# Three unread products in the idle rounds of the even mixer's hand-woven stages

## The chip, the cores and the metric

The kernel runs on one core of one Trainium2 chip. The metric is the device time in microseconds; the median of repeated runs counts. The engines are TensorE (PE in the profile; PEld is its weight loads), VectorE (DVE), ScalarE (ACT), GpSimd (POOL) and SyncE (SP, which issues most DMAs).

## What is computed

A two-layer backbone over 256 context and 256 latent tokens of width 1024. Layer 0 (even) mixes with RWKV-7 in two directions beside a pooling mixer; layer 1 (odd) with differential attention beside retention. Behind each stands a mixture of 32 gated experts, two per token. The change lies in the even mixer, whose core is this, per head and direction:

```python
def step(S, inp):
    w_t, k_t, v_t, kk_t, b_t = inp[:5]
    sa = jnp.einsum('bhvk,bhk->bhv', S, -kk_t)
    S = S * w_t[:, :, None, :] + sa[..., None] * b_t[:, :, None, :] + v_t[..., None] * k_t[:, :, None, :]
    return S, jnp.einsum('bhvk,bhk->bhv', S, inp[5])
```

Before it the token rows are projected (h @ w_in), shifted and gated; after it come a norm per head, a bonus term, a gate and the output projection.

## The kernel before

All is float32, and nearly all matmuls are plain float32. The even mixer does not scan token by token. It cuts the 512 tokens into eight chunks of 64 and handles two halves of four heads each, in two directions, so there are four units (half, direction). A unit has three steps. `ev_prep` (products at L690, L697, L703, L743 and L752) builds the decayed matrices of every chunk. `ev_solve` (L802, L825) inverts the triangular blocks with many products of 32 rows, 32 columns and 32 elements. `ev_chain` (L871 to L903) carries the state through the eight chunks, three yields for a chunk.

Beside these run projections of weights (`ev_k`, `ev_r`, `ev_v`, `ev_u`, all at L545) and pieces of the adaLN table (`ev_ada`, L269 to L291), which depend on nothing but weights that a ring buffer streams in.

The order of all this is written out by hand. Each step is a Python generator that emits some instructions and yields. `STAGES` is a table of eight entries: the main generators, the fill generators, a rate `per`, and the PSUM banks for fill and for aside products. `weave` (L109) goes round: each main generator once, then as many steps of fill as the rate has made due. Entries are woven one after the other (L447 to L450). Where the fill of an entry has run out, `next(fill, None)` does nothing and the round holds main work alone. A `per` below 1 gives rounds without fill; the last entry's fill outlasts its main generators.

The yields that matter for a count: an `ev_ada` piece has 3, `ev_k`, `ev_r` and `ev_v` 8 each, `ev_turn` 2, `ev_u` 16. `ev_prep` has 26 yields, so it is in its 27th round when it ends; `ev_chain` has 24, `ev_solve` 25.

The fill's first bank is called f; among the stages' generators only fill writes to it. Every engine takes its instructions in the order in which they were emitted, so what is emitted in one round stands on TensorE ahead of what is emitted in the next. `ident` is a 128x128 identity matrix that is loaded once at the start.

The stages of the odd layer are woven by the same function (L1217 to L1237). The expert layer that follows the even mixer streams its weights from HBM.

Of the kernel before, what the change touches and what calls it, by code (L numbers as in the profile page):

```python
# [10 lines left out]
F32 = mybir.dt.float32  # L11
# [94 lines left out]
    return where, arrays  # L106


def weave(main, fill=(), per=1):  # L109

    fill, end, due, main = chain(*fill), object(), 0, list(main)
    while main:
        main = [g for g in main if next(g, end) is not end]
        due += per
        while due >= 1:
            next(fill, None)
            due -= 1
    for _ in fill:
        pass
# [87 lines left out]
class Kernel:  # L207
# [182 lines left out]
    def even(self, xp, seg):  # L390

        nc, tc, I, c = self.nc, self.tc, self.I, self.c
        with ExitStack() as st:
            self.adaw = mp = st.enter_context(tc.tile_pool(name="even", bufs=1))
            self.xp, self.mp = xp, mp
            unit = ExitStack()
            self.up = unit.enter_context(tc.tile_pool(name="unit", bufs=2, side="right"))

            parts = [self.up.tile([128, 8, *shape], F32R, name=n) for n, *shape in
                     (("AB", 8, 64), ("RK0", 2, 64), ("RK1", 2, 64), ("tok0", 128), ("tok1", 128))]  # L400
            parts = [a.rearrange("p a s i -> p (a s i)" if len(a.shape) == 4 else "p a i -> p (a i)") for a in parts]
            parts = [a[:, n:n + 512] for a in parts for n in range(0, a.shape[1], 512)]
            self.hH, self.hL = parts[:8], parts[8:]
            with ExitStack() as s1:
                tp = s1.enter_context(tc.tile_pool(name="evp", bufs=1))
                self.pp = s1.enter_context(tc.tile_pool(name="evpp", bufs=1, space=PSUM))
                self.bank = self.bank_of("fgh")
                self.condition(mp, tp)
                x = self.inputs(tp, nc.sync)
                first = s1.enter_context(tc.tile_pool(name="first", bufs=5))  # L410
                self.stream.early = first, 9, 5
                self.stream.fill()
                hT = self.x_tiles(xp, [2, 512])
                self.hT = [hT[k // 2][:, k % 2] for k in range(8)]
                mix = self.mix_in(tp, self.pp, 0, x, self.cols[0], 5)
                next(mix)
                pieces = [self.ada(*next(self.todo)) for n in range(4)]
                for n in range(5):
                    if n < 4:
                        next(pieces[n])  # L420
                        next(pieces[n])
                    if n == 0:
                        next(mix)
                    if n == 1:
                        parameters = self.parameters(tp)
                        next(parameters)
                        self.constants(mp, "even", ("heads", "upto0", "mask0", "upto1", "mask1", "eye16", "sub2", "subcol", "headsel", *(f"headrow{t}" for t in range(4))))
                        self.constants(mp, "even", [f"sel{i}" for i in range(16)])
                        self.stream.fill()
                    if n == 3:  # L430
                        lora = self.lora(first)
                        next(lora)
                    if n:
                        next(pieces[n - 1])
                next(mix)
                next(lora)
                next(parameters)
            self.hp = st.enter_context(tc.tile_pool(name="half", bufs=1))
            self.wp = st.enter_context(tc.tile_pool(name="evw", bufs=1))
            self.pp = st.enter_context(tc.tile_pool(name="evps", bufs=1, space=PSUM))  # L440
            self.VU = [self.hp.tile([128, 4, 4, 64], F32, name=f"VU{j}") for j in range(2)]
            self.yT01, yT23 = (mp.tile([128, 2, 512], F32, name=f"yT{b}") for b in range(2))
            self.yT = [a[:, b] for a in (self.yT01, yT23) for b in range(2)]
            self.half, self.unit, self.done, self.seg = {}, {}, set(), seg
            self.splits_ = self.ev_splits()
            self.ahead = list(islice(self.splits_, 2))
            self.free_units = unit.close  # L447
            for main, fill, per, banks, aside in self.STAGES:
                self.bank, self.aside = self.bank_of(banks), self.bank_of(aside)
                weave([getattr(self, "ev_" + n)(*a) for n, *a in main], [getattr(self, "ev_" + n)(*a) for n, *a in fill], per)  # L450
        return self.x

    def bank_of(self, names):
# [219 lines left out]
    def ev_prep(self, half, d):  # L673
# [12 lines left out]
        for q in range(2):  # L686
            b = 2 * half + q
            ps = bank([128, 4, 128])
            for t in range(4):
                nc.tensor.matmul(ps[:, t], self.wdT[:, 128 * t:128 * t + 128], self.wup[:, d, 128 * b:128 * b + 128],  # L690
                                 start=t == 0, stop=t == 3, skip_group_check=True)
# [4 lines left out]
            ps = bank([128, 512])  # L696
# [4 lines left out]
            ps = bank([128, 512])  # L701
            for t in range(4):
                nc.tensor.matmul(ps[:, 128 * t:128 * t + 128], lw[:, t], c[f"upto{d}"], start=t == 0, stop=t == 3,  # L703
                                 skip_group_check=True)
# [35 lines left out]
            for n in range(2):  # L740
                ps = bank([128, 4, 128])
# [4 lines left out]
            for n in range(2):  # L746
                for h in range(2):
                    H = slice(64 * h, 64 * h + 64)
                    ps = bank([128, 4, 128])
                    for i in range(4):  # L750
                        ch = 4 * n + i ^ q
                        nc.tensor.matmul(ps[:, i], KB[H, 128 * ch:128 * ch + 128], u["RK"][q][H, ch].rearrange("p s i -> p (s i)"),  # L752
                                         start=i == 0, stop=i == 3, skip_group_check=True)
# [2 lines left out]
                    yield  # L756
        for h in range(2):
            nc.vector.tensor_scalar(u["PH"][:, :, :, h], u["Pe"], c["heads"][:, 64 * h:64 * h + 1], None, op0=ALU.mult)

    def ev_solve(self, half, d):  # L760

# [420 lines left out]
    def odd(self, x, seg):  # L1182

        nc, tc, I = self.nc, self.tc, self.I
        with ExitStack() as st:
# [28 lines left out]
            for g in (self.od_turned("k0", self.kT[0:2], 0), self.od_turned("q0", self.qT[0:2], 256), self.od_tokens("v0", self.V[0])):  # L1214
                for _ in g:
                    pass
            weave([*(self.od_attend(n, 0) for n in range(2)), self.router_weights(self.bank_of(("b6",)))],  # L1217
                  [self.od_turned("k1", self.kT[2:4], 0), self.od_turned("q1", self.qT[2:4], 256), self.od_tokens("v1", self.V[1])], 2)
            self.flush()
            weave([*(self.od_attend(n, 1) for n in range(2)), self.od_heads(0, self.Yr[0], self.ss[0], 1e-5)],  # L1220
                  [self.od_turned("dk", self.dkT, 0), self.od_turned("dq", self.dqT, 256), self.od_tokens("dv0", self.DV[0])], 2)
            self.flush()
# [1377 lines left out]
```

## Time and profile before

| | us |
|---|---|
| median of three runs | 1868.96 |
| lowest, highest | 1865.75, 1869.52 |
| profiled execution, its own time | 1874.16 |
| span from its first to its last instruction | 1872.4 |
| TensorE busy | 1637.9 (87% of the span) |
| VectorE busy | 817.3 (44%) |
| ScalarE busy | 447.0 (24%) |
| mean granted TensorE clock | 0.925 |

The span is what all positions in the profile are counted in, in microseconds from the first instruction. [...] A matmul's time in the profile is from its start until its result is out, and matmuls overlap, so a busy TensorE may still have room; the distance from one group's start to the next one's tells how long it holds the engine. The even mixer goes from about 50 to about 575 us.

### The profile page before, as it was taken

Reading aid. Unit: us, or ns where it says so; the run is one execution under the profiler, and the core shown is the slowest. Engines: PE = TensorE matmul, PEld = TensorE weight load, DVE = VectorE, ACT = ScalarE, POOL = GpSimd, SP = SyncE. Lnnn points to the kernel's source line nnn. Section 1 sums busy time; section 2 is a strip of 40 time slices with the busy share of each in tenths; the row PEclk is TensorE's granted clock in tenths of the full one; section 3 lists DMA queues with packets and bytes.
Section 4 is the critical chain, followed back from the end, with each engine's and each line's share of the span. In section 5 each row is a group of like instructions: output and inputs, shape, how many; then the busy total and the mean of one; then the engine's idle time right before and its main releaser. Section 6 shows DMA issues by size and latency. Waiting matters only on the chain. (4 is left out here: it accounts for less than half of the span.)

```text
span 1872.4 us, 31604 instructions
## 1 busy us (share of the span) xinstructions
PE 1637.9 (87%) x12958; PEld 933.3 (50%) x12958; DVE 817.3 (44%) x1622; ACT 447.0 (24%) x945; POOL 139.5 (7%) x170
## 2 busy tenths in 40 slices
PE   5988999989998999999999997999987787776667
PEld 2755556454776444444444433888754333332222
DVE  2564434544358245555555456665562212221113
ACT  3442222421213211111111112544421111111001
POOL 1021000103115000000000003200010000000001
PEclk8998987879898999999999997999988899898888
DMA  9275300652243879999999990622699998999996
GB/s 319 82 239 191 113 24 23 216 172 92 85 146 141 350 283 386 399 385 390 390 401 379 399 386 12 198 68 85 259 369 413 415 415 318 414 414 414 366 400 253
DMA packets 127284, 505.76 MB, mean 270 GB/s; under 512 B 11317, under 2 KB 38945, under 8 KB 85986
## 3 DMA queue, kind: packets, MB, share of 16 engines
q1 hardware_dynamic: 120946, 493.96, 68.1%
q0 software_dynamic: 3488, 8.26, 1.4%
q8 instruction: 143, 2.34, 0.5%
q10 hardware_dynamic: 2640, 0.65, 0.2%
q14 instruction: 67, 0.55, 0.1%
HBM read 501.73 MB, written 1.10 MB: 269 GB/s over the span
## 5 line engine op out<-in xcount | busy, mean ns | idle before, releaser
L1979 PE MATMUL b<-w,ht 128*64 128x512 f32 x512 | 118.8, 604 | 8.6 <-PEq L2197 8.2
L2004 DVE TENSOR_TENSOR tmp<-b,g 128x512 f32<-128x512 f32 x128 | 87.6, 686 | 70.1 <-PE b L2002 69.2
L1958 PE MATMUL b<-w,xh 128*64 128x512 f32 x512 | 116.9, 599 | 0.0
L1958 PE MATMUL b<-w,xg 128*64 128x512 f32 x512 | 116.9, 599 | 0.0
L2287 PE MATMUL b<-w,x 128*32 128x256 f32 x1024 | 77.8, 430 | 31.7 <-DMA w<-moe_w_up 14.9
L2006 DVE TENSOR_TENSOR x<-x,tmp 128x512 f32<-128x512 f32 x124 | 90.1, 726 | 4.3
L2287 PE MATMUL b<-w,xg 128*32 128x256 f32 x1024 | 74.0, 420 | 19.1 <-DMA w<-moe_w_up 14.4
L1987 DVE TENSOR_TENSOR yl<-b,yh 64x512 fp32r<-64x512 f32 x62 | 42.7, 688 | 101.4 <-ACT yh L1986 101.4
L2304 PE MATMUL b<-w,ht 128*32 128x256 f32 x1024 | 71.2, 415 | 16.6 <-ACT ht L2299 12.4
L2292 DVE SCALAR_TENSOR_TENSOR low<-b,gs,low 64x256 f32<-64x256 f32 x32 | 15.7, 490 | 157.6 <-ACT low L2291 157.6
L1979 PEld LDWEIGHTS b<-w,ht 128*64 128x64 f32 x512 | 41.6, 138 | 84.0 <-issue 72.5
L1962 ACT ACTIVATE low<-b 64x512 f32<-64x512 f32 x33 | 19.4, 588 | 253.9 <-PEq L2197 221.0
L2453 DVE COPY y<-b 32x256 f32<-32x256 f32 x62 | 25.9, 418 | 119.6 <-PE b L2304 106.3
L2287 PEld LDWEIGHTS b<-w,x 128*32 128x32 f32 x1024 | 37.1, 122 | 69.5 <-DMA w<-moe_w_up 20.6
L1986 ACT CAST yh<-b 64x512 fp32r<-64x512 f32 x62 | 36.0, 581 | 127.8 <-PE b L1979 104.6
L1963 DVE SCALAR_TENSOR_TENSOR low<-b,gs,low 64x512 f32<-64x512 f32 x32 | 36.1, 1127 | 67.2 <-ACT low L1962 67.2
L1958 PEld LDWEIGHTS b<-w,xh 128*64 128x64 f32 x512 | 33.9, 136 | 62.6 <-issue 62.0
L1958 PEld LDWEIGHTS b<-w,xg 128*64 128x64 f32 x512 | 33.9, 136 | 62.3 <-issue 61.3
L2291 ACT ACTIVATE low<-b 64x256 f32<-64x256 f32 (+1 forms) x36 | 14.4, 399 | 209.9 <-PEq L2501 130.4
L2287 PEld LDWEIGHTS b<-w,xg 128*32 128x32 f32 x1024 | 36.0, 120 | 53.3 <-DMA w<-moe_w_up 19.5
L2002 PE MATMUL b<-yh,oht 128*128 128x512 f32 (+1 forms) x128 | 58.3, 456 | 3.2 <-DVE tmp L2004 3.2
L1374 PE MATMUL b<-w,hH 128*128 128x256 f32 x320 | 59.4, 286 | 0.0
(868 smaller groups left out, 3115.5 us busy)
## 6 DMA issues: line engine op xcount, KB each, us to landing
w<-moe_w_gate SPq DMA_DIRECT2D x128, 1024.0 KB
w<-moe_w_up SPq DMA_DIRECT2D x128, 1024.0 KB
w<-moe_w_down SPq DMA_DIRECT2D x128, 1024.0 KB
w<-ada_w SPq DMA_DIRECT2D x48, 1024.0 KB
w<-od_w_in SPq DMA_DIRECT2D x12, 1024.0 KB
w<-ev_w_in SPq DMA_DIRECT2D x8, 1024.0 KB
w<-ev_w_out SPq DMA_DIRECT2D x5, 1024.0 KB
w<-od_w_out SPq DMA_DIRECT2D x4, 1024.0 KB
```

What stands on the lines that cost most here:

```text
L1374: nc.tensor.matmul(ps[:, t], l[:, k, T], r[:, k], start=t == 0 and k == 0 and i == 0, stop=k == 7 and i == 2, skip_group_check=True)
L1958: nc.tensor.matmul(ps[64 * j:64 * j + 64], xe(k), w[j][:, k % 4], start=k == 0, stop=k == 7)
L1963: nc.vector.scalar_tensor_tensor(hs[64:128].rearrange("s k q -> s q k"), ps[64:128].rearrange("s (q k) -> s q k", k=4), gs, sg[64:128].rea ...
L1979: nc.tensor.matmul(ps[64 * j:64 * j + 64], ht[:, k], w[:, k % 2, 512 * j:512 * j + 512], start=k == 0, stop=k == 3)
L1986: nc.scalar.copy(out=yh[:, j], in_=pj)
L1987: nc.vector.tensor_tensor(yl[:, j], pj, yh[:, j].bitcast(F32), op=ALU.subtract)
L2002: nc.tensor.matmul(ps, ohT[0:n, t], y[0:n, j], start=i == 0, stop=i == len(parts) - 1)
L2004: nc.vector.tensor_tensor(tmp, ps, g2[seg[t]][:, 512 * j:512 * j + 512], op=ALU.mult)
L2006: (nc.gpsimd if j in aside else nc.vector).tensor_tensor(xs, xs, tmp, op=ALU.add)
L2287: nc.tensor.matmul(ps[groups[j]], xe(k), w[j // 2][:, k % 4, 256 * (j % 2):256 * (j % 2) + 256], start=k == 0, stop=k == 7, skip_group_che ...
L2304: nc.tensor.matmul(ps[groups[j]], ht[:, k % 2, S * (k // 2):S * (k // 2) + S], w[:, k % 2, 256 * j:256 * j + 256], start=k == 0, stop=k == ...
L2453: (nc.scalar.copy if j % 2 else nc.vector.tensor_copy)(out=out, in_=ps[groups[j]])
```

## The change

`weave` gets a function `idle`. It is called where a step of fill is due, the fill has run out, and a main generator is left. For the even mixer's entries it is `ev_idle`, which takes bank f and issues three products of the identity with itself, 128 columns each, into it; nothing reads them. For the entry that has `end` among its main generators, and for the odd layer's stages, it does nothing.

```diff
-def weave(main, fill=(), per=1):
+def weave(main, fill=(), per=1, idle=lambda: None):
...
         while due >= 1:
-            next(fill, None)
+            if next(fill, end) is end and main:
+                idle()
             due -= 1
...
-                weave([getattr(self, "ev_" + n)(*a) for n, *a in main], [getattr(self, "ev_" + n)(*a) for n, *a in fill], per)
+                weave([getattr(self, "ev_" + n)(*a) for n, *a in main], [getattr(self, "ev_" + n)(*a) for n, *a in fill], per,
+                      self.ev_idle if ("end",) not in main else lambda: None)
...
+    def ev_idle(self):
+
+
+        ps = self.pp.tile([128, 512], F32, name="f")
+        for i in range(3):
+            self.nc.tensor.matmul(ps[:, 128 * i:128 * i + 128], self.c["ident"], self.c["ident"], start=i == 0, stop=i == 2, skip_group_check=True)
```

## Rows read from the trace of the kernel before

**Rows 1.** The page's second part: granted clock and DMA share, 40 slices

```profile
PEclk8998987879898999999999997999988899898888
DMA  9275300652243879999999990622699998999996
```

**Rows 2.** Busy time, granted clock, DMA share and GB/s by stretch

```profile
core 0: us, PE busy (x) PEld busy (x) DVE busy (x) ACT busy (x) POOL busy (x), PEclk, DMA share, GB/s
165.00:171.80 6.80, 4.07 (x97) 2.60 (x101) 5.07 (x11) 1.09 (x2) 0.00 (x0) 0.50 0.38 144
178.60:192.20 13.60, 13.60 (x183) 9.24 (x184) 7.03 (x14) 4.96 (x10) 0.36 (x2) 0.50 0.11 27
257.20:270.70 13.50, 12.19 (x139) 7.49 (x133) 2.10 (x4) 5.48 (x9) 0.00 (x0) 0.50 0.06 21
308.40:339.00 30.60, 29.84 (x145) 19.46 (x145) 11.78 (x25) 8.45 (x18) 1.21 (x3) 0.50 0.18 61
383.50:403.80 20.30, 19.03 (x305) 13.92 (x305) 7.50 (x14) 6.64 (x13) 0.57 (x2) 0.50 0.24 81
468.80:485.70 16.90, 15.68 (x217) 11.20 (x211) 3.69 (x8) 7.12 (x14) 4.46 (x7) 0.50 0.51 154
485.90:574.50 88.60, 87.28 (x611) 64.70 (x610) 48.74 (x91) 16.21 (x37) 18.57 (x17) 1.00 0.29 101
575.00:1120.00 545.00, 528.82 (x2624) 250.37 (x2625) 270.55 (x449) 101.40 (x188) 16.42 (x12) 0.98 0.91 364
```

**Rows 3.** Timeline of TensorE: start, length, line, shapes; products and transposes of 128 columns

```profile
118.45 0.66 PE L743 MATMUL p<-const_ident,KB 128*128 128x128 f32 x4 [0.46 <-DVE KB L726]
118.94 0.60 PE L743 MATMUL P<-const_ident,KB 128*128 128x128 f32 x4
...
157.33 1.16 PE L703 MATMUL P<-const_heads,lw 128*128 128x128 f32 x8
158.42 0.99 PE L802 MATMUL s<-A,const_sel 32*32 32x224 f32 x16
...
336.97 1.92 PE L703 MATMUL p<-const_heads,lw 128*128 128x128 f32 x8
338.68 1.14 PE L280 MATMUL c<-const_ident,part 128*128 128x2 f32 x8
```

**Rows 4.** The same timeline, 167 to 183 us; in brackets idle time before, and releaser

```profile
167.73 2.07 PE L920 MATMUL C<-sq,const_heads 128*128 128x512 f32 x2 [3.71 <-DVE sq L916]
...
177.98 0.37 PE L752 MATMUL p<-RK,KB 64*128 64x128 f32 x1 [1.63 <-issue]
...
181.28 2.07 PE L752 MATMUL p<-RK,KB 64*128 64x128 f32 x8
```

**Rows 5.** The same timeline, 254 to 271 us

```profile
254.44 0.33 PE L903 MATMUL y<-AB,VU 128*64 128x64 f32 x2 [0.69 <-ACT VU L884]
...
259.41 1.92 PE L825 MATMUL s<-TT,A 32*32 32x32 f32 x64 [1.31 <-ACT A L845]
...
266.50 3.78 PE L545 MATMUL f<-x,w 128*128 128x512 f32 x4
```

**Rows 6.** The same timeline, 293 to 309 us

```profile
293.70 1.16 PE L752 MATMUL p<-RK,KB 64*128 64x128 f32 x8
294.79 0.46 PE L890 MATMUL C<-VU,tok 128*64 128x64 f32 x8
...
305.96 0.65 PE L890 MATMUL C<-VU,tok 128*64 128x64 f32 x6 [1.09 <-ACT VU L884]
...
308.53 0.70 PE L874 MATMUL c<-ZB,RK 128*64 128x128 f32 x4 [1.18 <-DVE ZB L897]
```

**Rows 7.** The same timeline, breaks and waits around 384 and 468 us

```profile
384.77 1.49 PE L825 MATMUL s<-TT,A 32*32 32x32 f32 x93 [4.23 <-issue]
...
468.11 0.50 PE L825 MATMUL s<-TT,A 32*32 32x32 f32 x35 [3.24 <-issue]
...
477.57 1.92 PE L825 MATMUL s<-TT,A 32*32 32x32 f32 x64 [0.69 <-ACT A L845]
...
480.64 1.05 PE L883 MATMUL C<-R,AB 64*64 64x64 f32 x8 [0.53 <-ACT R L876]
```

## The prediction

> **What bounds the kernel now.** I read the page's slices first. In the first eleven the granted TensorE clock dips again and again while the DMA engines are mostly idle; later the DMA engines are 0.9 busy and more [rows 1]. The even mixer is the first part, so there TensorE and its clock set the pace, and the expert layer behind it, 0.91 busy with DMA, can only start when the mixer has ended [rows 2]. I therefore count a microsecond won or lost in the mixer as one at the end.
>
> Second, the table by stretch, cut where the clock changes [rows 2]. [...]
>
> Third, TensorE's timeline ahead of each fall. The first has a 3.71 us wait for VectorE in front of it, the second a 1.63 us break in which TensorE waited for nothing that the profile shows [rows 4]. The third has waits of 0.69 and 1.31 us around it [rows 5], the fourth waits of 1.09 and 1.18 us [rows 6], the fifth and sixth breaks of 4.23 and 3.24 us [rows 7]. So a fall follows a short hole, and the slow stretch then outlasts the hole by far.
>
> **Where the products go.** I counted the yields. A triple is issued in each round in which the fill has run out and a main generator is left. Entry 2 of STAGES has 27 rounds at 0.8 and 19 fill steps: 1 triple. Entry 3: 27 rounds, 18 steps: 8. Entry 4: 26 and 22: 3. Entry 5: 27 rounds at 0.9 and 8 steps: 15. Entry 6: 27 and 23: 3. Entry 7: 26 and 22: 3. Entries 1 and 8: none. That is 33 triples, 99 products. Nothing is removed or moved, no DMA is added, and bank f was read out a round or more before the first triple of each entry, so no new wait arises. TensorE's queue is in order, though: all that is queued behind a triple is late by its length unless it would have waited anyway.
>
> **The price of one triple.** Four products of this shape appear as eight records and hold TensorE from 157.33 to 158.42, 1.09 us at the full clock; four one-record transposes of 128 columns are followed 0.49 us later by the next four without a gap [rows 3]. Six records cost 0.73 us by the transposes; the group with its closing gap gives 0.82 us for six, and 1.09 us is an upper end. A triple waits for nothing, so it should join the work around it without that gap. I take 0.70, just under the nearest row, with 0.65 and 1.09 as ends. At the half clock the four products take 1.71 us [rows 3], so a triple 1.3 to 1.5; I take 1.4.
>
> **What a held clock is worth.** The same group of eight records lasts 2.07 us at half clock and 1.16 us at full [rows 4, 6]. Work that keeps TensorE busy at half clock thus gives back 0.91 of 2.07, some 0.42 to 0.44 of its time; I use 0.42.
>
> **Entry 2**, one triple near 124 us at full clock. Whether TensorE is late there I did not follow up; +0.3, between 0 and 0.7.
>
> **Entry 3**, eight triples between 164 and 187 us. The first lies in the 3.71 us wait: free. That hole is still some 3 us long, so I let the first fall stand, and the second triple costs 1.4. Six follow at full clock, 4.2, of which I hide 1.5 in the break of 1.63 us [rows 4]. Cost 4.1. Since they stand on both sides of the break, I expect the fall at 178.6 not to come: 0.42 of 13.6 busy us is 5.7 [rows 2]. Net -1.6.
>
> **Entry 4**, three triples between 253 and 261 us. Two lie in the waits of 0.69 (nearly all of it) and 1.31 us [rows 5]; the third costs 0.7. The fall at 257 should not come, since the holes that led to it are filled: 0.42 of 12.19 is 5.1. The large group in it, 3.78 us long [rows 5], can shrink fully, as it waits for nothing. Net -4.4.
>
> **Entry 5**, fifteen triples between 294 and 326 us, is the balance on which the sum hangs. Up to 305 the groups stand back to back: eight records of the preparation from 293.70, the chain's next piece at 294.79, 1.09 us later [rows 6]. Six triples there delay everything. Two lie in the waits of 1.09 and 1.18 us. Seven more follow among back-to-back work. Thirteen paid at 0.70 are 9.1. Against it, the fall at 308 should not come: 0.42 of 29.84 is 12.5. If it stayed away without cover from ScalarE and VectorE, up to 1.5 of this would turn into waits for them, and they would be late next. Net -3.4.
>
> **Entry 6**, three triples behind 392 us. The 4.23 us break comes in a round that still has fill, so nothing is put there and the fall at 383.5 stands; the triples run at half clock, 4.2, and may bring the clock back a little earlier. I take 1.0 for that, between 0 and 0.42 of 10 us. Net +3.2. **Entry 7**: the 3.24 us break is ahead of its triples too. They cost 4.2, of which 1.2 goes into waits of 0.69 and 0.53 us [rows 7]; an earlier rise gives 1.6. Net +1.4.
>
> Sum: 0.3 - 1.6 - 4.4 - 3.4 + 3.2 + 1.4 = -4.5 us. The profiled execution took 1874.16 us for a span of 1872.4, 5.2 us above the median of 1868.96; it would become 1869.7, and the median 1864.5.
>
> [...] The breaks come in front of small products with many instructions each, and a triple adds instructions ahead of them, so a break may move to a better or worse place; from the rows, each is worth between nothing and 4.23 us [rows 7]. The sum leaves them where they are. [...]
>
> **Rivals.**
> *Slower: the clock falls at 178.6 all the same.* Then seven triples of entry 3 are paid at 1.4, 9.8 less 1.5, and nothing comes back: -1.6 becomes +8.3, the sum +5.4, 1874.4 us. For it: a 1.63 us break alone, between busy groups, was enough before, and 32x32 products fill much of that time. Against: a triple stands on each side. It decides from the point at which the clock there is below about 0.75. If the third fall stays too, -4.4 becomes about +2.1 and the time 1881.
> *No change: the triples fit worse.* At 1.09 each, some twenty paid at full clock add 7.8: +3.3, 1872.3; at about 0.9 they add 4 and leave -0.5, 1868.5. For it: every group in the rows has its gap behind it. Against: the transposes have none.
> *A larger gain: a break moves.* Without the fifth fall entry 6 goes from +3.2 to 2.1 less 8.0, -5.9, and the sum to -13.6: 1855.4 us. It hangs on a place that nothing in the change aims at.
> *The change does nothing to the clock* because products nobody reads are dropped, or never issued: 1869. The program writes them to a bank like any other; I give it next to nothing.
>
> **How the numbers follow.** Some 0.2%, 3.7 us, is what a measurement here tells from no change. The forecast, between -9 and 0, has 0.50: 0.34 of it below -3.7, 0.16 within. A worse fit 0.13, all within. A larger gain 0.10. The slower rival 0.27. That makes faster 0.44, same 0.29, slower 0.27. Both signs hold much of the chance; the forecast's own range is 1860 to 1869. The range for all reaches down to the moved break, 1855, and up between the two prices of the slower rival, 1878.
>
> **What would show it.** Right: 1.00 in the stretches that began at 178.6, 257.2 and 308.4; 0.50 again behind the breaks of entries 6 and 7; triples of 0.65 to 0.9 us at full clock; the work from 294 to 305 us longer by some 4 us. Wrong: a triple above 1 us; 0.50 in the fourth stretch, which alone turns -3.4 into a loss of more than 9; or full clock in entry 6.

## The result and the profile after

The changed kernel takes 1884.20 us, the median of six runs (1881.64 to 1890.17); the kernel before, run beside it, 1868.28. The ratio is 1.0086 (95% interval 1.0068 to 1.0103): **slower by 15.9 us**. I had forecast 1864.5 and a range up to 1878.

The page of the changed kernel, its profiled execution (1890.17 us, the slowest of the six):

```profile
span 1888.4 us, 32004 instructions
PE 1652.5 (88%) x13156; PEld 950.7 (50%) x13156; DVE 818.1 (43%) x1622; ACT 446.6 (24%) x945; POOL 140.2 (7%) x170
PEclk8999989979897999999999998999989999887878
q8 instruction: 144, 2.36, 0.5%
```

TensorE has 198 matmuls and 198 weight loads more than before (12958 of each). So the 99 products are 396 instructions: two matmuls and two loads each. In all the page counts 400 more than the 31604 of before; the other four are waits of TensorE on semaphores, in the mixer. The slices of the mixer show more nines than in [rows 1]: the clock is held better (0.931 against 0.925 over the whole kernel), and the kernel is slower all the same. The last slices (eights and nines down to 7878) are no better than before, though the change adds nothing there.

The stretches at 0.50 of the mixer, but for two of 3.4 us at 64.0 and 122.1, by stretch (PE busy, PEld, DVE, ACT, POOL, then granted clock as a share of the full one, DMA share, GB/s):

```profile
173.30:180.10 6.80, 6.01 (x141) 4.59 (x141) 3.59 (x7) 0.58 (x1) 0.00 (x0) 0.50 0.10 37
200.60:204.00 3.40, 3.40 (x38) 1.36 (x41) 0.38 (x2) 0.10 (x1) 0.00 (x0) 0.50 0.80 271
265.40:279.00 13.60, 13.23 (x113) 8.17 (x112) 2.10 (x4) 4.95 (x9) 0.00 (x0) 0.50 0.01 1
350.70:354.10 3.40, 3.40 (x16) 1.66 (x16) 3.29 (x8) 0.27 (x1) 0.57 (x1) 0.51 0.84 317
388.30:415.50 27.20, 24.05 (x350) 18.71 (x350) 7.87 (x14) 7.01 (x14) 0.87 (x2) 0.50 0.22 74
480.50:490.70 10.20, 8.24 (x94) 5.76 (x86) 1.70 (x3) 2.72 (x6) 4.47 (x7) 0.50 0.78 236
```

Against [rows 2]: the 30.6 us of the fifth entry are gone (3.4 left, later), the 13.6 us at 178.6 have become 3.4, the 13.5 us at 257 have stayed, the sixth entry's stretch has grown from 20.3 to 27.2, and the seventh's has shrunk from 16.9 to 10.2.

A triple, and TensorE's breaks, by its timeline (matmuls of `ev_idle` stand on L768, `ev_prep`'s on L746 and L755, the solver's small products on L835):

```profile
130.57 0.94 PE L768 MATMUL f<-const_ident 128*128 128x128 f32 x6
131.43 1.16 PE L755 MATMUL P<-RK,KB 64*128 64x128 f32 x8
...
175.95 1.49 PE L768 MATMUL f<-const_ident 128*128 128x128 f32 x6
177.23 1.06 PE L746 MATMUL p<-const_ident,KB 128*128 128x128 f32 x4
...
303.06 0.94 PE L768 MATMUL f<-const_ident 128*128 128x128 f32 x6
303.92 0.46 PE L900 MATMUL C<-VU,tok 128*64 128x64 f32 x8
...
389.65 1.93 PE L835 MATMUL s<-TT,A 32*32 32x32 f32 x128 [3.40 <-issue]
393.38 1.11 PE L746 MATMUL P<-const_ident,KB 128*128 128x128 f32 x4 [1.80 <-issue]
...
408.60 1.65 PE L768 MATMUL f<-const_ident 128*128 128x128 f32 x6
410.18 2.07 PE L755 MATMUL P<-RK,KB 64*128 64x128 f32 x8
...
479.63 0.96 PE L835 MATMUL s<-TT,A 32*32 32x32 f32 x88 [3.87 <-issue]
```

From the start of a triple to the start of what follows are 0.86 us at the full clock (twice above; the median of all 33) and 1.28 to 1.58 at half (both ends above; 1.58 four times). The breaks, in which TensorE waits for nothing that the profile shows, are not where they were in [rows 4, 7]: sizes and places have moved.

**Where the breaks stand.** I counted every record of TensorE from the start of the trace, those included that the busy columns leave out, up to each break of 0.7 us or more between 100 and 500 us. In the kernel before they come after 2241, 2497, 6849 and 8897 records; in the changed one after 7105, 7361, 9153 and 9409. The remainder modulo 256 is 193 in all of these, and in every one of 71 more such breaks in the eighteen kernels of the experiments. So breaks of this size come there only at every 256th record. I call these places **cuts**, and the 256 records between two of them a block; an inserted instruction moves all later cuts in the program. The 400 added move those behind the mixer by 400 - 256 = 144 places.

In the page's queue "q8 instruction" are 144 packets, 2.36 MB in all and 16.4 KB each. That TensorE waits for them at the cuts I infer from their times. In the kernel before, packets of the queue land at 172.80, 176.66, 383.46 and 466.71 us, and the four breaks end at 174.25, 177.98, 384.77 and 468.11. From the second break to the third, 4352 records, 17 packets land, one for every 256. All 79 breaks end 1.14 to 1.59 us behind a landing, though there are only some 35 landings in the 400 us. No two packets start less than 3.3 us apart there in any trace, while the 256 records ahead of the four breaks were used up in 2.36, 1.83, 2.70 and 2.68 us. In all traces 65 of the 79 breaks follow a block used up in less than 3.3 us, and only 35 of the 633 cuts without such a break do. So a cut shows as a break mostly where a block falls into dense small products that are through in less than the 3.3 us between two packets.

**The end of the kernel** shows the loss where nothing was added. The latest and longest of TensorE's waits for "issue" or its own sequencer (PEq) in the last 70 us; first the kernel before, then the changed one:

```profile
1842.48 0.41 PE L2311 MATMUL b<-const_ident,oh 128*128 128x128 f32 x2 [0.30 <-PEq L2501]
1850.49 3.67 PE L2518 MATMUL b<-y,oht 96*128 96x512 f32 x8 [0.31 <-PEq L2501]
```

```profile
1821.35 3.04 PE L2329 MATMUL b<-y,oht 128*128 128x512 f32 x6 [1.18 <-issue]
1857.30 0.41 PE L2321 MATMUL b<-const_ident,oh 128*128 128x128 f32 x2 [0.30 <-PEq L2511]
1862.46 3.21 PE L2297 MATMUL b<-w,x 128*32 128x256 f32 x51 [0.79 <-issue]
1866.49 3.67 PE L2528 MATMUL b<-y,oht 96*128 96x512 f32 x8 [0.81 <-PEq L2511]
```

The 19 waits of this kind of 0.7 us or more after 1790 us, in all traces, end 1.28 to 1.86 us behind the landing of an instruction packet.

From one and the same VectorE instruction (a `low` addition, L2292 before and L2302 after, at 1738.50 and 1751.22 us) to the end are 133.9 us before and 137.2 after. I call this the **end segment** below.

### The profile page after: what moved, and what is told of

It reads as the page before. It is cut to its first block, busy times and chain, and to the rows that moved or that the text cites. A ratio compares the mean times of both kernels' runs of the same rounds, so it can differ in the third digit from the quotient of the medians.

```text
span 1888.4 us, 32004 instructions
## 1 busy us (share of the span) xinstructions
PE 1652.5 (88%) x13156; PEld 950.7 (50%) x13156; DVE 818.1 (43%) x1622; ACT 446.6 (24%) x945; POOL 140.2 (7%) x170
## 3 DMA queue, kind: packets, MB, share of 16 engines
q8 instruction: 144, 2.36, 0.5%
## 5 line engine op out<-in xcount | busy, mean ns | idle before, releaser
L2297 PE MATMUL b<-w,x 128*32 128x256 f32 x1024 | 76.9, 419 | 29.2 <-DMA w<-moe_w_up 13.5
L2314 PE MATMUL b<-w,ht 128*32 128x256 f32 x1024 | 75.0, 430 | 17.3 <-ACT ht L2309 12.5
L2302 DVE SCALAR_TENSOR_TENSOR low<-b,gs,low 64x256 f32<-64x256 f32 x32 | 15.7, 491 | 147.4 <-ACT low L2301 147.4
```

The costliest lines, as they stand in the source:

```text
L2297: nc.tensor.matmul(ps[groups[j]], xe(k), w[j // 2][:, k % 4, 256 * (j % 2):256 * (j % 2) + 256], start=k == 0, stop=k == 7, skip_group_che ...
L2314: nc.tensor.matmul(ps[groups[j]], ht[:, k % 2, S * (k // 2):S * (k // 2) + S], w[:, k % 2, 256 * j:256 * j + 256], start=k == 0, stop=k == ...
```

## The experiments

Two theories at the outset: *cost*, by which the triples' own TensorE time is the loss, and *cuts*, by which it is the added instructions that move what follows. The expectations call *cost* theory A (and, where nothing at all is paid back by the clock, rival C), and *cuts* rival or theory B. Each kernel was timed beside the kernel before; differences are of medians (the kernel before had 1866.93, 1868.49, 1868.84, 1869.07 and 1867.94 us in the five batches).

### Parts of the change, shorter products, other operands

```diff
-                      self.ev_idle if ("end",) not in main else lambda: None)
+                      self.ev_idle if n_ in (4,) else lambda: None)
```

(the first kernel; `n_` counts the entries of STAGES from 0. The second has `(1, 2, 3, 5, 6)`. The third and fourth keep all entries and have another product:)

```diff
-            self.nc.tensor.matmul(ps[:, 128 * i:128 * i + 128], self.c["ident"], self.c["ident"], start=i == 0, stop=i == 2, skip_group_check=True)
+            self.nc.tensor.matmul(ps[0:32, 2 * i:2 * i + 2], self.c["ident"][0:32, 0:32], self.c["ident"][0:32, 0:2], start=i == 0, stop=i == 2, skip_group_check=True)
...
-            self.nc.tensor.matmul(ps[:, 128 * i:128 * i + 128], self.c["ident"], self.c["ident"], start=i == 0, stop=i == 2, skip_group_check=True)
+            self.nc.tensor.matmul(ps[:, 128 * i:128 * i + 128], self.c["ident"], self.gup[:, 128 * i:128 * i + 128], start=i == 0, stop=i == 2, skip_group_check=True)
```

> Triples in the fifth entry alone (15 of the 33). Theory A (the queue): a triple holds TensorE 0.86 us at full clock wherever other work is ready, and only in the fifth entry does a held clock pay that back; there the pair of traces gives -2.2 us. So -5 to 0 us against the kernel before. Rival B (the triples' instructions move the breaks, wherever they are issued): +5 to +12 us, since the fifth entry brings 180 of the 396 TensorE instructions and the breaks of the sixth and seventh entries are behind it. Rival C (the products lengthen every round, nothing is ever paid back): +8 us or more.

Measured: 1875.30, ratio 1.0038 (1.0021 to 1.0055), +8.4 us.

> Triples in the second, third, fourth, sixth and seventh entry, none in the fifth (18 of 33). Theory A: the losses of the change without its gain, +10 to +18 us against the kernel before, and 0.50 again in the fourth slow stretch. Rival B: about half of the change's loss, +5 to +9 us. Rival C: 18 of 33 of the loss, +7 to +9 us.

Measured: 1875.56, ratio 1.0042 (1.0029 to 1.0056), +8.6 us. Either half alone is slower. The first speaks against theory A, which had -5 to 0 there; between the rivals B and C the two don't decide, as both had what came.

> The same 33 triples with the same count of instructions, but of 32 rows, 32 columns and 2 moving columns: hardly any TensorE time and nothing for the clock. Theory A: the clock falls as in the kernel before, a triple costs a closing gap and little else, 0.2 to 0.5 us, some +4 to +9 us; the fifth entry pays and gets nothing back. Rival B: +12 to +18 us, as much as the change, since the instructions are all there.

Measured: 1886.78, ratio 1.0109 (1.0088 to 1.0131), +19.9 us. A triple of tiny products holds TensorE for 0.27 us where the change's holds it for 0.86:

```profile
297.16 0.34 PE L768 MATMUL f<-const_ident 32*32 32x2 f32 x6
297.43 0.46 PE L900 MATMUL C<-VU,tok 128*64 128x64 f32 x8
```

All 33 are then some 33 x 0.27 = 8.9 us, and the loss is twice that, more than either side expected: *cost* alone falls, since with a third of the TensorE time the loss did not shrink. The mean granted clock of its six runs, 0.920 against 0.926 in the kernel before, shows nothing held. The number of instructions is what the two kernels share.

> All 33 triples, with the identity as weights but real numbers (the gate parameters, 128 columns of them) as the moving operand. Rival D (products of an identity with itself count for little, since nearly all that moves are zeros, so the clock falls in the fourth entry and behind the breaks though the array is streaming): the clock stays at 1.00 in the fourth entry, 5 to 10 us less than the change. Theory A: what moves does not matter, within 3 us of the change, 0.50 in the fourth entry's end as before.

Measured: 1883.57, ratio 1.0092 (1.0069 to 1.0115), +16.6 us, as much as the change's 15.9: the operands made no difference in time that shows here. Its profile has no fall of the clock near 260 us, unlike the change's, which looked like a hint that real operands hold the clock better. Two later kernels take it back: with the identity and 29 products behind the mixer that fall is absent too, and with real operands in entries 4 and 5 it is there (first the one, then the other, columns as above):

```profile
257.00:271.00 14.00, 12.88 (x208) 8.86 (x210) 4.60 (x10) 6.46 (x11) 0.23 (x1) 1.00 0.17 59
```

```profile
263.40:277.10 13.70, 13.70 (x110) 8.93 (x106) 2.10 (x4) 5.48 (x9) 0.00 (x0) 0.50 0.01 3
```

### The shift by itself

The same tiny products stand at the start of the kernel, where TensorE waits for a DMA (8.96 us in the first trace): 35 of them in the kernel before (140 instructions, the change's 396 modulo 256), then 64 (256 instructions), then 29 in the changed kernel (396 + 116 = 512), and the kernel before as it is. The four semaphore instructions are not in these counts: 140 is four short of the change's shift, and the changed kernel with 29 ends four places off.

```diff
+                ps = self.pp.tile([128, 512], F32, name="f")
+                for i in range(35):
+                    self.nc.tensor.matmul(ps[0:32, 2 * i:2 * i + 2], self.c["ident"][0:32, 0:32], self.c["ident"][0:32, 0:2], start=i == 0, stop=i == 34, skip_group_check=True)
                 self.condition(mp, tp)
```

> The kernel before, with 35 small unread products (32 rows, 32 columns, 2 moving columns) ahead of TensorE's first work, where it waits 9 us and more for DMA. No triples. They are 140 TensorE instructions, and 396, the count of the change's 99 products, is 140 more than 256. [...] Theory A (the triples' own time): -2 to +2 us.

Measured: 1875.21, ratio 1.0035 (1.0016 to 1.0053), +6.7 us, more than theory A's -2 to +2.

> The same with 64 small products, 256 instructions, so that every cut falls where it does in the kernel before. Theory B: -2 to +2 us, and breaks of 4.2 and 3.2 us at the same instructions as before. If it is slow as well, the shift of the cuts is not the cause.

Measured: 1869.48, ratio 1.0010 (0.9994 to 1.0026).

> The change, with 29 small products at the start: 396 + 116 = 512 instructions, so behind the even mixer every cut falls where it does in the kernel before, while inside the mixer the cuts lie elsewhere. Theory B, if the cuts behind the mixer matter: the loss shrinks from 16 to 5 to 10 us. Theory A: 16 us as in the change.

Measured: 1867.84, ratio 1.0003 (0.9983 to 1.0023), better than the 5 to 10 us of loss that I expected. **The loss of 15.9 us is gone with every triple still in place.**

> The kernel before, unchanged, as a kernel of its own. All theories: the ratio's interval holds 1. Its profile is a second execution to read the first one against: if the mixer's length or the slow stretches differ by some 5 us between the two, my terms, read from one execution, are uncertain by as much.

Measured: 1868.92, ratio 1.0004 (0.9989 to 1.0018).

So 35 products cost something and 64 nothing that can be measured: it is the shift, not the number. The last 70 us of the first and the third of these kernels show it as a wait:

```profile
1835.89 3.50 PE L2290 MATMUL b<-w,x 128*32 128x256 f32 x49 [0.74 <-issue]
1842.56 6.84 PE L2521 MATMUL b<-y,oht 96*128 96x512 f32 x8 [3.17 <-PEq L2504]
```

```profile
1846.28 0.41 PE L2324 MATMUL b<-const_ident,oh 128*128 128x128 f32 x2 [0.30 <-PEq L2514]
1853.59 3.67 PE L2531 MATMUL b<-y,oht 96*128 96x512 f32 x8 [0.33 <-PEq L2514]
```

### Mixer or behind it

The tiny products go behind the mixer instead, ahead of the router's first product of the first layer's expert part: 29 in the changed kernel, then in the kernel before 35; 35 at the start and 29 behind; 16; 48.

```diff
+            if L == 0:
+                ps = self.pp.tile([128, 512], F32, name="b5")
+                for i in range(29):
+                    nc.tensor.matmul(ps[0:32, 2 * i:2 * i + 2], c["ident"][0:32, 0:32], c["ident"][0:32, 0:2], start=i == 0, stop=i == 28, skip_group_check=True)
             self.keep_clock(3, x[0])
```

> The change whole, and 29 tiny products (32 x 32, 2 columns, 116 TensorE instructions) that nothing reads, ahead of the router's first kept-clock product of the first layer's expert part, so behind the mixer. In the mixer the breaks between two matmuls stay where the change put them; behind it every later break is back where the kernel before has it. Cuts theory: only what the change loses at the end of the kernel comes back, by the traces 3.5 us (last weights landed to the end: 19.8 us before, 23.3 with the change), so 1878 to 1882 us, and the last 60 us show no TensorE wait over 0.5 us. Rival A, nearly the whole loss arises behind the mixer: 1868 us, as with the 29 at the start. Rival B, alignment at the end is worth nothing: 1884 us.

Measured: 1874.05, ratio 1.0026 (1.0007 to 1.0045), +5.2 us: some 11 of the 16 us come back (by the two intervals 6 to 16), more than the 3.5 I had read from the end, less than all.

> The kernel before with 35 tiny products (140 instructions, what the change adds modulo 256) ahead of the router of the first layer's expert part: the mixer's cuts stay, all later ones move as with the change. If the part of the loss that lies behind the mixer comes of the cuts alone: the 10 us that 29 products behind the mixer gave back, so 1876 to 1880 us. Rival A, the shift costs in the mixer: 1869 us. Rival B, it takes the change's later arrival and the shift together: 1870 to 1874 us.

Measured: 1871.26, ratio 1.0023 (1.0005 to 1.0041), +2.2 us: not the 7 to 11 us of the cuts alone, but within rival B, by which it takes the change's later arrival and the shift together.

> The kernel before with 35 tiny products at the start and 29 behind the mixer: the cuts in the mixer move by 140 instructions, those behind it stand as before (256 together). If the mixer's cuts cost what 35 at the start alone cost (+6.5 us): 1875 us. If that lay behind the mixer: 1868 to 1870 us, or some 4 us less, since the mixer took 496.7 us in the trace with 35 at the start, and 500.5 in the null run's.

Measured: 1864.69, ratio 0.9979 (0.9964 to 0.9993), **4.4 us faster than before**, the better end of what I expected.

> The kernel before with 16 tiny products (64 instructions) behind the mixer. If the cuts of the kernel before stand luckily behind the mixer: 1872 to 1880 us, and the last 60 us show a TensorE wait over 0.5 us. Rival, only some shifts cost: 1867 to 1870 us.

Measured: 1870.70, ratio 1.0010 (0.9993 to 1.0026), +1.6 us, not to be told from none and less than the 3 us or more that I expected, though the wait at the end is there (3.7 us, last table).

> The kernel before with 48 tiny products (192 instructions) behind the mixer. If the cuts of the kernel before stand luckily behind the mixer: 1872 to 1880 us, as with 16. Rival, only some shifts cost: 1867 to 1870 us.

Measured: 1871.74, ratio 1.0020 (1.0007 to 1.0033), +2.7 us, just short of what I expected. By the last table the end of these two is 4.5 and 4.8 us longer; whether all of it comes through, the intervals don't settle.

Parts don't add up: the shift in the mixer alone gave -4.4 and behind it alone +2.2, both together +6.7. One reason is that the products behind the mixer are not free of effects. These rows run from the wait for `lg` to the expert part's first product of weights, in the kernel before itself, then with 35 and 29, then with 35 and 93 (the next section):

```profile
580.66 5.90 PE L1816 MATMUL b<-x,const_ident 128*128 128x512 f32 x6 [0.40 <-DVE lg L1744]
...
597.64 1.94 PE L1958 MATMUL b<-w,xg 128*64 128x512 f32 x8
```

```profile
578.59 3.25 PE L1804 MATMUL b<-const_ident 32*32 32x2 f32 x58 [0.40 <-DVE lg L1747]
...
594.19 1.94 PE L1965 MATMUL b<-w,xg 128*64 128x512 f32 x8
```

```profile
577.48 10.07 PE L1804 MATMUL b<-const_ident 32*32 32x2 f32 x186 [0.40 <-DVE lg L1747]
...
599.10 1.94 PE L1965 MATMUL b<-w,xg 128*64 128x512 f32 x8
```

That way takes 17.0 us without them, 15.6 with 29 and 21.6 with 93. So 29 save 1.4 us there and 93 cost 4.6. The thirteen traces without such products have 16.5 to 18.1 us, the four with 16 to 35 have 15.4 to 15.9.

### With the cuts at the end in their old place

Now 29 at the start with real operands; 19 at the start with triples in the fifth entry alone (180 + 76 = 256); 10 at the start with real operands in the fourth and fifth (216 + 40); the change with 35 at the start and 58 behind; and the kernel before with 35 and 93. The edits are those above.

> The change with a slice of real weights in place of the identity as the moving operand, and 29 tiny products at the start, so that the later breaks sit as in the kernel before. Theory that identity by identity keeps the clock less well than real data: the 13.7 us at 0.50 near 257 to 265 us go, worth by the records at both levels 13.7 x 0.42 = some 5.7 us at most and 3 to 5 on the path, so 1863 to 1865 us. Rival, operands don't matter: 1868 us, as with the identity.

Measured: 1866.11, ratio 0.9990 (0.9974 to 1.0006), -2.7 us, not to be told from none, and between the two sides.

> Fifteen triples in the fifth entry alone, 180 instructions, and 19 tiny products (76) at the start: 256 together, so that all behind the fifth entry is broken where it was before. The fifth entry without its 30 us at 0.50 was shorter by 2.2 us in the change's trace: 1866 to 1867 us where the kernel before takes 1868.9. Rival, price and clock cancel: 1868.9 us. Without the 19 this kernel took 1875.3, so anything under 1870 is once more the breaks.

Measured: 1870.03, ratio 1.0005 (0.9989 to 1.0022), +1.2 us: price and clock cancel.

> Triples with real weights as the moving operand in the fourth and fifth entries only (3 and 15, 216 instructions), and 10 tiny products (40) at the start: 256 together. Entry 4's 13.7 us and entry 5's 30 us at 0.50 both go and the entries where triples only cost (6 and 7: +5.2 and +1.3 us in the change's trace) are left as before: 1861 to 1866 us, faster than the kernel before. Rival, a held clock doesn't shorten the mixer because its VectorE chain sets the end: 1868 to 1870 us.

Measured: 1871.50, ratio 1.0013 (0.9995 to 1.0031), +2.7 us: no gain either. Its clock still fell at 263.4 (row above), so the premise of the expectation held for the fifth entry alone.

> The change whole, with 35 tiny products at the start and 58 (232 instructions) behind the mixer: 140 + 396 + 232 = 768, so the end is cut as in the kernel before, and the mixer starts with its cuts 140 instructions on. If the change in itself is worth nothing: 1864 to 1869 us. If its triples cost 0.86 us each wherever no clock is gained: 1869 to 1874 us.

Measured: 1866.22, ratio 0.9995 (0.9978 to 1.0013), -1.7 us: the change in itself is worth nothing that shows.

> The kernel before with 35 tiny products at the start and 93 behind the mixer (372 instructions; 512 together): the cuts in the mixer as with 35 and 29, those behind the mixer as in the kernel before. Cuts theory: 1864 to 1866 us where the kernel before takes 1869, faster by 3 to 5 us. Rival, the 1864.7 us of 35 and 29 were the luck of one build among many: 1868 to 1870 us.

Measured: 1872.25, ratio 1.0023 (1.0007 to 1.0039), +4.3 us. Neither side had it: against the kernel before of each batch, 8.7 us more than with 29 behind, of which 6.0 (21.6 less 15.6) are the products' own way. The remaining 2.7 lie within what the medians scatter. Whether the 4.4 us gain of 35 and 29 would hold in another build is therefore open; it is the one version measured that beats the kernel before clear of its interval.

All together, by the places by which the end is shifted (modulo 256, semaphore instructions included), the end segment of the profiled execution, and the longest wait of TensorE for issue or sequencer after 1790 us (waits of one line summed):

```
kernel                        shift  ratio    end segment  wait at the end
kernel before, again            0    1.0004      133.9          0.3
64 at the start                 0    1.0010      132.3          0.3
change, 29 at the start         4    1.0003      132.5          0.3
change, 29 behind               4    1.0026      132.6          0.3
real operands, 29 at the start  4    0.9990      130.1          0.3
entry 5 alone, 19               1    1.0005      132.4          0.3
entries 4 and 5, 10             2    1.0013      132.1          0.3
35 at the start, 29 behind      0    0.9979      133.6          0.3
35 at the start, 93 behind      0    1.0023      132.9          0.3
change, 35 and 58               4    0.9995      133.7          0.3
the change                    144    1.0086      137.2          1.2
tiny triples                  144    1.0109      140.3          2.4
real operands                 144    1.0092      139.0          2.4
35 at the start               140    1.0035      139.3          3.2
35 behind                     140    1.0023      135.9          3.1
entry 5 alone                 181    1.0038      136.8          4.0
all but entry 5               219    1.0042      141.6          3.4
16 behind                      64    1.0010      138.4          3.7
48 behind                     192    1.0020      138.7          3.7
```

The two groups don't overlap in the end segment: 132.6 us on average with the cuts in their old place or up to four from it, 138.6 without. **The kernel before happens to have its cuts at the end where they show as no more than 0.3 us**; every other shift tried costs there. How far the cuts are from each other at the end I can't show by the count as in the mixer, since there the remainders differ; but 35 products at the start and 35 behind the mixer put the two waits after the same records, with 0.74 and 0.82, 3.17 and 3.10 us.

## Why the prediction was wrong

**The step that failed** is "The sum leaves them where they are", said of the breaks, and with it "all that is queued behind a triple is late by its length", taken as all that it can cost. I had seen the breaks and had named added instructions as what may move them, but priced this at nothing, looked no further than the mixer, and made of it a rival only on the gaining side. The runs put it at 11 to 17 us: the ratio is 1.0086 for the change as it is, and 1.0003, 1.0026 and 0.9995 for the change with the cuts of the end put back. Of the 16 lost, the end segment holds 3.3 in the change's trace against the kernel before, 3.5 to 4.7 against its three realigned forms. With 29 behind the mixer some 11 us came back, and 2 of them may be those products' own saving (the way from `lg` took 18.0 us in the change's trace, 15.9 there). Some 4 us behind the mixer and the rest within it are not located: the mixer took 496.0 to 514.7 us in the profiled executions of the change and its realigned forms, so a single trace doesn't resolve it. Why the change loses 16 us to a shift of 144, where one of 140 costs the kernel before 2 to 7, is open.

**The count** of 33 triples was right: 198 matmuls at six records each.

**The price** was too low: 0.86 us, not 0.70, so 33 x 0.16 = 5.3 us more if all are on the path. I had the group "with its closing gap" at 0.82 and argued the gap away; it was there. At half clock it was 1.28 to 1.58 (above), around the 1.4 I took.

**The held clock** came as the sum wanted, and gave too little. My rate of 0.42 is for queued work, and TensorE was busy in 94.4 of the 101.7 us of the six stretches at 0.50 in [rows 2]. The stretches at half clock that begin between 100 and 595 us add up to 116.1 us in the kernel before, 81.9 in the change, and 47.8 with real operands and 29 at the start. The last is 68.3 us less, worth 68.3 x 0.42 = 28.7 us at my rate; the price is 33 x 0.86 = 28.4. Two sums of the same size: the mixer took 496.0 us there against 500.5 in the repeated kernel before. Over all runs of a kernel, too, the clock rises and the time does not fall: the mean granted clock is 0.924 in the repeated kernel before and 0.937 in the change with 29 at the start, at a ratio of 1.0003.

**Entry by entry**, between the same VectorE instructions, change against the profile of before. These are single executions, and the change's is the slowest of its six. The change with 29 behind has the same instructions in its mixer with the same cuts, and its profile is the fastest of twelve: 499.0 us for the mixer, 30.7 of them at half clock, against 514.7 and 71.7. The 41 us less at half are worth 17 at my rate, so the rows that follow, +10.4 in sum, hold how often the clock happened to fall. Entries 1 and 2 (+0.3): +4.2, though one triple is all that is new there; the repeated kernel before has +1.6 without any. Entry 3 (-1.6): +0.6; the fall at 178.6 stayed away as forecast, so the rival that wanted it was not what made the kernel slower. Entry 4 (-4.4): +1.3, as the fall at 265 came; in the three kernels where it did not come (real operands, with and without 29, and the change with 29 behind) the stretch took 82.5 us against 87.0: -4.5 where -4.4 was forecast. Entry 5 (-3.4): -2.1, sign right; but the repeated kernel before took 63.6 us there where its first profile took 66.3 and the change 64.2, so the typical gain is none, as the kernel with the fifth entry alone and 19 says. The kernel with triples everywhere but here shows the two terms apart: the clock was held without them (6.8 us at half against 27.3 in the repeated kernel before), and the entry took 56.1 us. So by these traces the held clock is worth 7.5 us, not 12.5, and the fifteen triples cost some 8, not 9.1. Entry 6 (+3.2): +5.2, its stretch at 0.50 being longer by 6.9 us. Entry 7 (+1.4): +1.2.

**The frame**, that a microsecond in the mixer is one at the end, is not contradicted: from a VectorE instruction at the mixer's end to one well behind the first expert layer are 754.7 us before and 753.8 after, so that part moved as a whole. What I had left out is that the last part is cut anew too.

## What to carry to other kernels

Added instructions can cost more than their time: on TensorE here they move every later cut of its stream, and 35 products hidden in a wait were worth +6.7 us. Before judging a small change, run the kernel before with the same number of idle instructions put where the engine waits, and the change padded up to a full distance between cuts (256 records in these traces; 64 products, 256 instructions, gave 1.0010); what then remains is the change's own, but for the cuts between the two places. And where an edit trades a fixed price against a gain that comes and goes with the clock (here 30.7 and 71.7 us at half clock with the same instructions and cuts in the mixer), read the gain from several executions of the kernel before, not from one.

## What the runs showed that I had not expected

- Breaks of TensorE in the mixer stand 256 records apart or a multiple of it: all 79 of at least 0.7 us, in the twenty traces, at the same remainder, each ending 1.14 to 1.59 us behind the landing of an instruction packet; up to 4.7 us long. The longest in the kernel before and in the change (4.23 and 3.24, 3.87 and 3.40 us) stand where the cut falls into dense small products (the solver's, [rows 7]).
- 35 tiny products in a wait of 8.96 us at the start, free in themselves, made the kernel 6.7 us slower; 64 in the same place did nothing measurable.
- 29 tiny products ahead of the router made its way shorter by 1.4 us: the four-record groups that follow last 0.63 us with them, some 1.05 without, at a granted clock of 1.00 against 0.50.
